# Hymba hybrid layer: the low parts of split weights from GpSimd to VectorE, SiLU as one ScalarE function, and the gate weights' split by ScalarE and VectorE

## The chip, the core and the metric

The kernel runs on one core of a Trainium2 chip. The core has a matrix engine (TensorE, PE in the profile, with its weight loads as PEld), three engines for elementwise work (VectorE, DVE; ScalarE, ACT; GpSimd, POOL), and SyncE (SP), whose queue issues nearly all DMA transfers here. Each engine works through its own queue in the order of the program and waits on semaphores for the others. The metric is the time of one execution on the device in microseconds (us), lower is better. The kernel before takes 1418.91 us, the median of three runs from 1418.45 to 1420.51.

## The reference

One decoder layer over 2048 positions of width 1024. The input `x` is RMS-normalised and multiplied by `w_in` (1024 x 6144). The six blocks of 1024 columns feed two mixers, a gated short convolution and a linear recurrence (RG-LRU); each output is normalised by heads, multiplied by the SiLU of its own gate block, and both together go through `w_out` (2048 x 1024), a residual addition and a last RMSNorm. All is float32.

```python
proj = jnp.einsum('bsd,de->bse', xn, w_in)
b_gate, c_gate, x_conv, g_conv, x_lru, g_lru = jnp.split(proj, splits, axis=-1)
y_conv = b_gate * causal_depthwise_conv(c_gate * x_conv, conv_w)
y_conv = headwise_rms_norm(y_conv, N_CONV_HEADS, conv_out_g) * jax.nn.silu(g_conv)
# rg_lru_mixer: u = conv(x_lru) + b
r = sigmoid(einsum('bshd,hde->bshe', uh, w_a) + b_a); i = sigmoid(einsum(..., w_i) + b_i)
log_a = 8.0 * r * log_sigmoid(lam); a = exp(log_a)
h_t = a_t * h_{t-1} + sqrt(-expm1(2 * log_a_t)) * (i_t * u_t)
y_lru = headwise_rms_norm(h, N_LRU_HEADS, lru_out_g) * jax.nn.silu(g_lru)
h = x + jnp.einsum('bse,ed->bsd', concat(y_conv, y_lru), w_out)
return rms_norm(h, final_g)
```

## The kernel before

**Products.** Each large product is done as a 2 x 2 block product with seven block products in place of eight (Winograd's form of Strassen's algorithm). So the weights of a step become seven combined blocks `S_0` to `S_6` (sums and differences of four loaded pieces `raw`), and the normalised activations, once per half of the sequence, seven combined blocks `T`. For precision each block is split in two: a high part, a cast to the matrix engine's fp32r format (`s` for weights, `th` for activations), and a low part, the float32 value less its high part (the second half of the `s` tile, and `tl`). A block product is then `sh*th + sh*tl + sl*th`, three matmuls for each of four pieces of depth: 12 matmuls of 128x512 (`mm`, L886), the **slot** in which the program is laid out.

**Steps.** The program goes through steps `n`, each of seven slots: for each block `k` of 128 columns an `l` step (`x_lru` and `g_lru`, consumer `lru`), an `a` step (`c_gate`, `x_conv`, `conv_a`) and a `b` step (`b_gate`, `g_conv`, `conv_b`); 24 steps for the first half of the sequence, 24 for the second, then 16 `o` steps for the output projection. Three steps `l`, `a`, `b` are called a period here. In steps 4 to 23 the split weights are also stored to DRAM (`sd`, L202), and the second half loads them again (`s_loads`, L218).

**The order.** The order on every engine is written by hand: instructions stand in the queues in the order in which the Python code makes them. `at(slots, f)` puts a function off by so many slots, `tick()`, called once a slot, runs those that are due. `s_plan` gives the eight pieces of work that make the next step's `S` blocks, one of which is done in each slot: `add` (a sum on VectorE), `hi` (ScalarE's cast, L197), `lo` (the low part, through `low` and `tt`, L160). In steps 4 to 23 (`PLAIN < n < 3 * KT`) the low parts 0, 4 and 6 are GpSimd's, the other four VectorE's. The store of a block follows its low part, by 3 slots where GpSimd made it and by 2 where VectorE did.

**Around the recurrence.** In `lru`, `sth` and `stl` split `u` into the tile `st`, `gates` lets TensorE multiply it by the split gate weights `bh` and `bl` into two small banks (`gate`, L666), `sigs` takes four sigmoids of them (L673) into `r` and `i`, for the first 512 columns and then for the second, which need the same two banks. Then come `tanh` (L682), `exp` (L685), a square root (L688), two products and the scan (L700). ScalarE holds one table set of functions at a time: sigmoid and tanh are in one, `exp` and the square root each need another, and the program has an ACT_TABLE_LOAD ahead of a function whose set isn't there.

**The SiLU.** `silu(g)` takes the sigmoid of a gate block into `sg` (ScalarE, L599) and two slots later multiplies it on GpSimd. `finish` later multiplies the normalisation gain, the mixer's output and this gate (L570). `load_gate_w` loads the gate weights and splits them with two GpSimd instructions (L615, L616).

**The banks.** The accumulated sums of a step lie in banks of PSUM, and ScalarE copies them out (`q`, `u`, `rr`, L1220 to L1226) or VectorE adds them to what was copied; the bank is free for TensorE after that. `u` (u2) is one tile, written again in each step, so its copy waits until VectorE has used the last one, which it does where it makes the last quarter of `gb` or `gl`.

Of the kernel before, what the change touches and what calls it, by code (L numbers as in the profile page):

```python
# [12 lines left out]
F32 = mybir.dt.float32  # L13
F32R = mybir.dt.float32r
AF = mybir.ActivationFunctionType
ALU = mybir.AluOpType
# [7 lines left out]
KT = D // P  # L24
# [14 lines left out]
def hymba_kernel(ctx: ExitStack, tc: tile.TileContext, x, xt, w_in, par, lamc, w_gate, w_out, final_g, out):  # L39
    nc = tc.nc  # L40
# [16 lines left out]
    sd = [dram.tile([7, P, 2, C], F32, name=f"sd{n}") for n in range(3 * KT)]  # L57
# [4 lines left out]
    def wt(tag, name, n=2 * C, dt=F32, bufs=1):  # L62
        return work.tile([P, n], dt, tag=tag, bufs=bufs, name=name)

    IG, O2, HL = 2, 2, 4
# [4 lines left out]
    def aux(name):  # L70
        return small.tile([P, C], F32, tag="aux", bufs=4, name=name)
# [69 lines left out]
    def at(slots, *fs):  # L141
        if slots == 0:
            for f in fs:
                f()
        else:
            due.append([slots, fs])
# [12 lines left out]
    def tt(out, a, b, op, eng=None):  # L159
        (eng or nc.vector).tensor_tensor(out=out, in0=a, in1=b, op=op)  # L160
# [6 lines left out]
    def low(v, hl, eng=None):  # L167
        tt(hl[1], v, hl[0].bitcast(F32), ALU.subtract, eng)
# [7 lines left out]
    def s_plan(n, r, dst):  # L176
        a11, a12, a21, a22 = r
        t, tiles = {}, {}

        def add(i):  # L180
            if i == 2:
                t[2] = aux("s1")
                tt(t[2], a21, a22, ALU.add)
            elif i == 1:
                t[1] = aux("s2")
                tt(t[1], t[2], a11, ALU.subtract)
            elif i == 3:
                tt(a21, a11, a21, ALU.subtract)
            else:
                tt(t[1], a12, t[1], ALU.subtract)  # L190

        def val(i):
            return {0: a11, 1: t.get(1), 2: t.get(2), 3: a21, 4: a12, 5: t.get(1), 6: a22}[i]

        def hi(i):
            tiles[i] = s_tile(dst, i)
            nc.scalar.copy(dst[i][0], val(i))  # L197

        def lo(i, eng=None):
            low(val(i), dst[i], eng)  # L200
            if PLAIN <= n < 3 * KT:
                at(3 if eng else 2, lambda: nc.sync.dma_start(sd[n][i], tiles[i].bitcast(F32)))  # L202

        g = nc.gpsimd if PLAIN < n < 3 * KT else None
        return [lambda: (add(2), add(1)),
                lambda: (hi(0), lo(0, g), add(3)),
                lambda: hi(1),
                lambda: (hi(3), lo(1)),
                lambda: (hi(2), lo(3), add(5)),
                lambda: (hi(4), lo(4, g), lo(2)),  # L210
                lambda: hi(5),
                lambda: (hi(6), lo(6, g), lo(5))]


    def s_loads(src, dst):
# [6 lines left out]
    PLAIN = 3  # L222
# [7 lines left out]
    class TPrep:  # L230
# [3 lines left out]
        def add(self, i):  # L234
            b11, b12, b21, b22 = (self.r.get(n) for n in range(4))
            t = self.t
            if i == 2:
                t[2] = aux("t1")
                tt(t[2], b12, b11, ALU.subtract)
            elif i == 1:  # L240
                t[1] = aux("t2")
                tt(t[1], b22, t[2], ALU.subtract)
            elif i == 3:
                tt(b12, b22, b12, ALU.subtract)
            else:
                tt(t[1], b21, t[1], ALU.subtract)
# [23 lines left out]
        def val(self, i):  # L270
            b11, b12, b21, b22 = (self.r.get(n) for n in range(4))
            return {0: b11, 1: self.t.get(1), 2: self.t.get(2), 3: b12, 4: b21, 5: b22,
                    6: self.t.get(1)}[i]

        def hi(self, i, v=None):
            self.dst[i, self.j] = hl = t_tile(self.dst, i, self.j)
            nc.scalar.copy(hl[0], self.val(i) if v is None else v)

        def lo(self, i, eng=None, v=None):
            low(self.val(i) if v is None else v, self.dst[i, self.j], eng)  # L280
# [311 lines left out]
        at(d0 + 7, lambda: hl_done(2))  # L592

    def silu(g, late=0):
        sg = [None]

        def f1():
            sg[0] = wt("ig", "sg", bufs=IG)
            nc.scalar.activation(out=sg[0], in_=g, func=AF.Sigmoid)  # L599

        at(2 + late, f1)
        at(4 + late, lambda: tt(g, g, sg[0], ALU.mult, nc.gpsimd))

# [2 lines left out]
    def load_gate_w(k):  # L608
        bd = aux("bd")[:, 0:2 * P].rearrange("p (h m) -> p h m", h=2)
        bh = small.tile([P, 2, P], F32R, tag="bh", name="bh")  # L610
        bl = small.tile([P, 2, P], F32R, tag="bl", name="bl")
        nc.sync.dma_start(bd, w_gate[k])

        def part():
            nc.gpsimd.tensor_scalar(out=bh, in0=bd, scalar1=1.0, scalar2=0.0, op0=ALU.mult, op1=ALU.add)  # L615
            nc.gpsimd.tensor_tensor(out=bl, in0=bd, in1=bh.bitcast(F32), op=ALU.subtract)  # L616

        at(3, part)
        return bh, bl
# [299 lines left out]
    g = nc.gpsimd  # L919
    with tc.manual_schedule(engines={ENG.PE, ENG.Activation, ENG.DVE, ENG.Pool, ENG.SP}):  # L920
# [176 lines left out]
        for n in range(PLAIN, N):  # L1097
# [53 lines left out]
            for s in range(8 if new or last else 7):  # L1151
                i = ((0, 6) + ORDER[1:])[s]
# [131 lines left out]
```

## Time and profile before

| | |
|---|---|
| median of three runs | 1418.91 us (1418.45 to 1420.51) |
| span of the profiled execution | 1418.1 us |
| TensorE, matmuls | 5732, mean 395 ns for 128x512 with `th` |
| VectorE busy | 1069.9 us |
| ScalarE busy | 782.6 us |
| GpSimd busy | 242.6 us, of it 118.9 in 62 low parts of weights (1931 ns each) and 87.6 in 32 products of the SiLU |
| ACT_TABLE_LOAD | 54 of 1283 ns |

The profile is of one execution; its span runs from the first to the last instruction, and nothing that is shown gives that execution's own time apart from it. The median of the runs lies 0.8 us above this span. A row of the time views has the start in us, the duration in us, engine, line, operation, output and inputs, shapes and count, and in brackets how long the engine had been idle and what ended that; a merged row (x2) has the time of all its instructions. A row of the waits view reads: who waited, for whom, us in total, times, longest. Matmuls overlap, and their listed durations are longer than the distance of their starts.

### The profile page before, as it was taken

To read this page: it belongs to the slowest core of one execution; us is meant where nothing else is said; L and a number is where in the kernel's file an instruction comes from. 1 tells how busy PE (TensorE), PEld (TensorE's weight loads), DVE (VectorE), ACT (ScalarE), POOL (GpSimd) and SP (SyncE) were. 2 spreads that over 40 slices of the span, in tenths; PEclk is the share of its full clock that TensorE was granted. 3 is DMA by queue.
4 is the path that set the end of the run, shared out by engine and by line. 5 is a ranking of instruction groups with operands and counts; after the bars stand their busy time and mean duration, and the time that the engine had idled before them with its cause. 6 is when DMAs were issued, how large, how long until landed. Compare 5 with 4: busy or idle time off the path is not lost.

```text
span 1418.1 us, 16977 instructions
## 1 busy us (share of the span) xinstructions
PE 1336.5 (94%) x5732; PEld 1072.3 (76%) x5732; DVE 1069.9 (75%) x1273; ACT 782.6 (55%) x1165; POOL 242.6 (17%) x159
## 2 busy tenths in 40 slices
PE   6989999999999997899998999998996999988997
PEld 5867777778777775677886878786874888867886
DVE  6778788898989989777767667665667647657885
ACT  7485757666566666375563645463656323343443
POOL 2104333433534430101000000101010000000000
PEclk9999999999999998999999999999997999999999
DMA  5147797898888865730899999998979998697643
GB/s 213 30 141 256 274 280 212 310 326 284 310 280 293 315 242 198 240 97 30 291 315 339 331 339 333 368 294 302 300 259 340 352 304 260 223 390 284 214 155 144
DMA packets 165191, 371.02 MB, mean 262 GB/s; under 512 B 17265, under 2 KB 52465, under 8 KB 165105
## 3 DMA queue, kind: packets, MB, share of 16 engines
q1 hardware_dynamic: 164816, 369.63, 76.3%
q8 instruction: 45, 0.74, 0.2%
q14 instruction: 42, 0.34, 0.1%
q10 hardware_dynamic: 288, 0.32, 0.1%
HBM read 224.45 MB, written 145.43 MB: 261 GB/s over the span
## 4 chain that ended last, share of the span: by engine, by line
PE 65%; DMA 13%; ACT 9%; DVE 8%; issue 3%; SPq 2%; POOL 0%; DVEq 0%; ACTq 0%; POOLq 0%
PE bank L886 60%; PE norm_ps L559 2%; DMA sd<-s 2%; ACT i L673 2%; ACT r L673 2%; PE gate L666 2%; DMA s<-so 2%; DVE s L160 2%; DVE tl L160 1%; DMA yd<-gl 1%; DMA zr<-rsd 1%; DVE traw L160 1%; DMA raw<-in_w_in_dram 1%; DMA traw<-in_w_out_dram 1%; DMA raw<-yd 1%
## 5 line engine op out<-in xcount | busy, mean ns | idle before, releaser
L886 PE MATMUL bank<-th,s 128*128 128x512 f32 x3608 | 1147.0, 395 | 41.5 <-DMA s<-so 9.8
L886 PEld LDWEIGHTS bank<-th,s 128*128 128x128 f32 x3608 | 685.3, 190 | 204.4 <-ACT u L1223 12.2
L886 PE MATMUL bank<-tl,s 128*128 128x512 f32 x1804 | 710.5, 394 | 6.3 <-DVE tl L160 6.0
L886 PEld LDWEIGHTS bank<-tl,s 128*128 128x128 f32 x1804 | 342.9, 190 | 81.4 <-DVE tl L160 10.4
L160 POOL TENSOR_TENSOR s<-raw,s 128x512 fp32r<-128x512 f32 x62 | 118.9, 1931 | 256.4 <-ACT s L197 180.2
L197 ACT CAST s<-raw 128x512 fp32r<-128x512 f32 x136 | 81.8, 616 | 59.6 <-PE bank L886 43.4
L1223 ACT COPY u<-bank 128x512 f32<-128x512 f32 x58 | 34.0, 587 | 141.3 <-PE bank L886 90.9
L160 DVE TENSOR_TENSOR s<-s,s 128x512 fp32r<-128x512 f32 x102 | 103.5, 1015 | 5.4 <-ACT s L197 5.4
L160 DVE TENSOR_TENSOR tl<-traw,th 128x512 fp32r<-128x512 f32 x102 | 70.0, 711 | 47.5 <-ACT th L454 29.1
L160 POOL TENSOR_TENSOR gb<-gb,sg 128x1024 f32<-128x1024 f32 x16 | 41.8, 2611 | 351.4 <-ACT sg L599 331.4
L160 DVE TENSOR_TENSOR s<-raw,s 128x512 fp32r<-128x512 f32 (+1 forms) x120 | 89.8, 771 | 9.9 <-ACT s L197 5.3
L1220 ACT COPY q<-bank 128x512 f32<-128x512 f32 x58 | 33.8, 583 | 79.2 <-PE bank L886 74.2
L160 DVE TENSOR_TENSOR raw<-raw,zr 128x512 f32<-128x512 f32 x64 | 49.6, 801 | 29.6 <-DMA zr<-rsd 29.6
L197 ACT CAST s<-s 128x512 fp32r<-128x512 f32 x102 | 62.8, 616 | 5.9 <-DVE s L160 5.9
L640 DVE SCALAR_TENSOR_TENSOR u<-xl,pt,u 128x1024 f32<-128x1024 f32 x48 | 64.5, 1344 | 0.8 <-ACT u L636 0.2
L1226 ACT COPY rr<-bank 128x512 f32<-128x512 f32 x58 | 33.9, 584 | 47.8 <-PE bank L886 47.7
L160 DVE TENSOR_TENSOR st<-u,st 64x1024 fp32r<-64x1024 f32 x32 | 52.0, 1626 | 1.0
L750 DVE SCALAR_TENSOR_TENSOR t<-p,pt,t 128x1024 f32<-128x1024 f32 x32 | 47.6, 1486 | 4.9 <-ACT t L747 4.1
L160 POOL TENSOR_TENSOR gl<-gl,sg 128x1024 f32<-128x1024 f32 x16 | 45.8, 2862 | 20.1 <-ACT sg L599 20.1
L160 DVE TENSOR_TENSOR ob<-bank,rr 128x512 f32<-128x512 f32 x18 | 12.2, 689 | 48.0 <-ACT rr L1226 48.0
L636 ACT ACTIVATE u<-xl,pt 128x1024 f32<-128x1024 f32 x16 | 19.9, 1245 | 46.8 <-DVE xl L160 46.8
L673 ACT ACTIVATE r<-gate,pt 64x512 f32<-64x512 f32 x64 | 43.8, 684 | 2.4 <-PE gate L666 1.8
(162 smaller groups left out, 1355.9 us busy)
## 6 DMA issues: line engine op xcount, KB each, us to landing
sd<-s SPq DMA_DIRECT2D x147, 512.0 KB, 4.8
s<-sd SPq DMA_DIRECT2D x147, 512.0 KB, 5.9
raw<-in_w_in_dram SPq DMA_DIRECT2D x108, 256.0 KB, 5.0
so<-so SPq DMA_DIRECT2D x42, 512.0 KB, 6.0
s<-so SPq DMA_DIRECT2D x42, 512.0 KB, 7.5
raw<-yd SPq DMA_DIRECT2D x64, 256.0 KB, 5.4
traw<-in_w_out_dram SPq DMA_DIRECT2D x56, 256.0 KB, 5.9
yd<-gl SPq DMA_DIRECT2D x32, 256.0 KB, 3.6
```

Source lines behind the costliest of these rows:

```text
L160: (eng or nc.vector).tensor_tensor(out=out, in0=a, in1=b, op=op)
L197: nc.scalar.copy(dst[i][0], val(i))
L559: nc.tensor.matmul(norm_ps[0], sel[:, s0:s0 + R], q[:, i * C:(i + 1) * C], start=norm_ps[1] == 0, stop=norm_ps[1] == 8 * KT - 1)
L636: nc.scalar.activation(out=v["u"], in_=o1[:, 1:1 + N2], func=AF.Identity, scale=lw[0], bias=pt[:, LB + k:LB + k + 1])
L640: nc.vector.scalar_tensor_tensor(out=v["u"], in0=o1[:, 1 + j:1 + j + N2], scalar=lw[j], in1=v["u"], op0=ALU.mult, op1=ALU.add)
L666: nc.tensor.matmul(ps[j], v["gw"][n][:, j, :], v["st"][j][:, sl], start=(n == 0), stop=(n == 1))
L673: nc.scalar.activation(out=g_[hi, sl], in_=v["ps"][j][src], func=AF.Sigmoid, bias=pt[src, bias + k:bias + k + 1])
L750: nc.vector.scalar_tensor_tensor(out=tcur["t"], in0=p[:, 2 + j:2 + j + N2], scalar=cw[j], in1=tcur["t"], op0=ALU.mult, op1=ALU.add)
L886: nc.tensor.matmul(bank, a[:, js], b, start=start and n == 0, stop=stop and n == 2, skip_group_check=more)
L1220: nc.scalar.copy(q1, bk["A"])
L1223: nc.scalar.copy(u2, bk["A"])
L1226: nc.scalar.copy(rr, bk["A"])
```

## The change

Three edits, all of which take work off GpSimd:

1. `lo` in `s_plan` is always VectorE's, so 60 low parts (0, 4 and 6 in steps 4 to 23) move from GpSimd to VectorE, and their stores to `sd` are issued 2 slots behind them and not 3.
2. `silu` is one ScalarE function in place, `Silu`; the tile `sg` and GpSimd's product go.
3. The gate weights' high part is a ScalarE cast and the low part a VectorE subtraction.

```diff
-        def lo(i, eng=None):
-            low(val(i), dst[i], eng)
+        def lo(i):
+            low(val(i), dst[i])
             if PLAIN <= n < 3 * KT:
-                at(3 if eng else 2, lambda: nc.sync.dma_start(sd[n][i], tiles[i].bitcast(F32)))
+                at(2, lambda: nc.sync.dma_start(sd[n][i], tiles[i].bitcast(F32)))
 
-        g = nc.gpsimd if PLAIN < n < 3 * KT else None
         return [lambda: (add(2), add(1)),
-                lambda: (hi(0), lo(0, g), add(3)),
+                lambda: (hi(0), lo(0), add(3)),
                 lambda: hi(1),
                 lambda: (hi(3), lo(1)),
                 lambda: (hi(2), lo(3), add(5)),
-                lambda: (hi(4), lo(4, g), lo(2)),
+                lambda: (hi(4), lo(4), lo(2)),
                 lambda: hi(5),
-                lambda: (hi(6), lo(6, g), lo(5))]
+                lambda: (hi(6), lo(6), lo(5))]
...
     def silu(g, late=0):
-        sg = [None]
-
-        def f1():
-            sg[0] = wt("ig", "sg", bufs=IG)
-            nc.scalar.activation(out=sg[0], in_=g, func=AF.Sigmoid)
-
-        at(2 + late, f1)
-        at(4 + late, lambda: tt(g, g, sg[0], ALU.mult, nc.gpsimd))
+        at(2 + late, lambda: nc.scalar.activation(out=g, in_=g, func=AF.Silu))
...
         def part():
-            nc.gpsimd.tensor_scalar(out=bh, in0=bd, scalar1=1.0, scalar2=0.0, op0=ALU.mult, op1=ALU.add)
-            nc.gpsimd.tensor_tensor(out=bl, in0=bd, in1=bh.bitcast(F32), op=ALU.subtract)
+            nc.scalar.copy(bh, bd)
+            tt(bl, bd, bh.bitcast(F32), ALU.subtract)
```

In the changed kernel the lines behind these edits have numbers that are 8 lower (the gate sigmoids are L665, the SiLU is L594).

TensorE's order is unchanged. ScalarE's queue around the gate sigmoids of an `l` step in the first half (`q` is the copy of a step's first bank, `p` a quarter of the next step's convolution input, `s` the high parts of weights), before:

```order
L729 COPY p<-bank 128x512
L197 CAST s<-s_2784 128x512
L1220 COPY q_2956<-bank 128x512
L673 ACTIVATE r<-gate,pt 64x512
L673 ACTIVATE i<-gate,pt 64x512
L673 ACTIVATE r<-gate,pt 64x512
L673 ACTIVATE i<-gate,pt 64x512
```

and after:

```order
L721 COPY p<-bank 128x512
L197 CAST s<-s_2769 128x512
L1212 COPY q_2938<-bank 128x512
L665 ACT_TABLE_LOAD
L665 ACTIVATE r<-gate,pt 64x512
L665 ACTIVATE i<-gate,pt 64x512
L665 ACTIVATE r<-gate,pt 64x512
L665 ACTIVATE i<-gate,pt 64x512
```

A table load stands between the copy of `q` and the first sigmoid. Such a load stands there in all 16 `l` steps, where before it stood in one, the first of the second half; the program has 69 loads in place of 54.

VectorE's queue around the scan of such a step (`s<-raw,s` and `s<-s_...,s` of 128x512 are low parts of weights, L691 and what follows belong to the recurrence, `xcol` is a normalised block of `x` for the second half), before:

```order
L691 SCALAR_TENSOR_TENSOR u<-r,u 128x1024
L160 TENSOR_TENSOR s<-s_2963,s 128x512
L160 TENSOR_TENSOR t<-bank,t 128x512
L160 TENSOR_TENSOR u<-T,u 128x1024
L700 SCALAR_TENSOR_TENSOR r<-r,u 128x1024
L703 COPY hl<-r 128x1
L520 SCALAR_TENSOR_TENSOR xcol<-xcol,pt 128x512
L160 TENSOR_TENSOR s_3146<-raw 128x512
L160 TENSOR_TENSOR s_3148<-s_3146,raw 128x512
L160 TENSOR_TENSOR gb<-bank,u_3014 128x512
L570 SCALAR_TENSOR_TENSOR gl<-r,pt,gl 128x1024
```

and after:

```order
L683 SCALAR_TENSOR_TENSOR u<-r,u 128x1024
L160 TENSOR_TENSOR s<-raw,s 128x512
L160 TENSOR_TENSOR s<-s_2946,s 128x512
L160 TENSOR_TENSOR t<-bank,t 128x512
L160 TENSOR_TENSOR u<-T,u 128x1024
L692 SCALAR_TENSOR_TENSOR r<-r,u 128x1024
L695 COPY hl<-r 128x1
L519 SCALAR_TENSOR_TENSOR xcol<-xcol,pt 128x512
L160 TENSOR_TENSOR s_3129<-raw 128x512
L160 TENSOR_TENSOR s_3131<-s_3129,raw 128x512
L160 TENSOR_TENSOR gb<-bank,u_2996 128x512
L569 SCALAR_TENSOR_TENSOR gl<-r,pt,gl 128x1024
```

One row is new within this stretch, the second, `lo(4)`; the others of a period's nine new low parts stand ahead of it and behind it.

## The prediction

> **What bounds the kernel now.** I read the page first, then who TensorE waits for, stage by stage, then the order of time around the gate sigmoids and around the scan, the two places that the diff touches.
>
> ```profile
> PE 1336.5 (94%) x5732; PEld 1072.3 (76%) x5732; DVE 1069.9 (75%) x1273; ACT 782.6 (55%) x1165; POOL 242.6 (17%) x159
> ```
>
> TensorE is busy 94% of the span, so another engine counts only where TensorE waits for it. The waits of TensorE from 104 to 530 us (steps 4 to 23, where GpSimd makes the low parts):
>
> ```profile
> PE bank L886 <- ACT u L1223: 4.6, 7, 1.0
> PE bank L886 <- ACT rr L1226: 1.7, 4, 1.2
> PE gate L666 <- ACT i L673: 1.2, 7, 0.2
> ```
>
> and from 700 to 990 us (second half of the sequence):
>
> ```profile
> PE norm_ps L559 <- DVE ql L160: 6.6, 4, 2.6
> PE bank L886 <- DMA s<-sd: 3.5, 4, 1.4
> PE bank L886 <- ACT q L1220: 2.8, 2, 1.4
> ```
>
> Two things are to be seen. In the first half TensorE waits 11 times for ScalarE's copies out of a bank, 6.3 us in all, and once in each period of three steps for the gate sigmoids. In the second half it loses twice as much, but for stores, loads and what hangs on them.
>
> **The new table load.** SiLU as one function isn't in the table set that holds the gate sigmoids: in the program order a load now stands in front of the first of them (none before, save once). The four sigmoids free the two small banks that the next gate matmuls need, and TensorE runs in order. A period without a load, ScalarE's copy first, then TensorE:
>
> ```profile
> 666.60 0.59 ACT L1220 COPY q<-bank 128x512 f32<-128x512 f32 x1 [2.58 <-PE bank L886]
> ...
> 668.90 0.39 PE L886 MATMUL bank<-th,s 128*128 128x512 f32 x1
> 669.94 0.50 PE L666 MATMUL gate<-st,bh 128*128 128x512 f32 x1 [0.18 <-ACT i L673]
> 670.51 0.39 PE L886 MATMUL bank<-th,s 128*128 128x512 f32 x1
> ```
>
> The copy waits for TensorE, the sigmoids follow it in ScalarE's queue, and the third row (0.18 us idle) shows that TensorE waits for the last of them already. So a load behind the copy has no cover: ScalarE's idle 2.58 us lie ahead of the copy, not behind it. And the trace holds the case with the load, once, because a square root has run in between:
>
> ```profile
> 603.79 0.59 ACT L1220 COPY q<-bank 128x512 f32<-128x512 f32 x1 [3.15 <-PE bank L886]
> 604.38 1.28 ACT L673 ACT_TABLE_LOAD   x1
> 605.68 0.68 ACT L673 ACTIVATE r<-gate,pt 64x512 f32<-64x512 f32 x1
> ...
> 606.04 0.39 PE L886 MATMUL bank<-th,s 128*128 128x512 f32 x1
> 607.12 0.50 PE L666 MATMUL gate<-st,bh 128*128 128x512 f32 x1 [0.69 <-ACT i L673]
> 608.52 0.50 PE L666 MATMUL gate<-st,bh 128*128 128x512 f32 x1 [0.67 <-ACT i L673]
> 609.09 0.39 PE L886 MATMUL bank<-th,s 128*128 128x512 f32 x1
> ```
>
> From the last matmul ahead of the gates to the first behind them TensorE needs 670.51 - 668.90 = 1.61 us without the load and 609.09 - 606.04 = 3.05 us with it: 1.44 us more. There are 16 `l` steps. One has the load already; in the very first,
>
> ```profile
> 79.58 0.68 ACT L673 ACTIVATE r<-gate,pt 64x512 f32<-64x512 f32 x1 [0.30 <-PE gate L666]
> ```
>
> ScalarE waits for TensorE just ahead of the sigmoids, and part of a load can run in that idle time; TensorE's wait list names none for `i` behind it. The other 14 pay: 14 x 1.44 = **+20.2 us**. The bounds of this term are 14 x 1.28 = 17.9 (the load alone) and 20.2.
>
> The Trainium skill ("ScalarE: Activation LUTs", What ACT_TABLE_LOAD costs) gives a switch of sets as 1283 ns and 1380 ns of drain, 2.66 us in all. By it the 14 loads would take 19 us more than I count and the forecast would be 1447; the trace has the 1.28 us, but no drain: the sigmoid starts 0.02 us behind the load at 605.66.
>
> **What GpSimd's work costs VectorE.** The scan stretch of a period in the first half, VectorE, then GpSimd and ScalarE, then two VectorE rows from moments without GpSimd:
>
> ```profile
> 351.24 0.68 DVE L160 TENSOR_TENSOR s<-s,s 128x512 fp32r<-128x512 f32 x1
> 352.44 2.15 DVE L160 TENSOR_TENSOR u<-T,u 128x1024 f32<-128x1024 f32 x1
> 354.62 2.29 DVE L700 TENSOR_TENSOR_SCAN r<-r,u 128x1024 f32<-128x1024 f32 x1
> 357.04 1.51 DVE L520 SCALAR_TENSOR_TENSOR xcol<-xcol,pt 128x512 f32<-128x512 f32 x1
> 358.47 1.77 DVE L160 TENSOR_TENSOR s<-raw 128x512 f32<-128x512 f32 x1
> 360.89 0.68 DVE L160 TENSOR_TENSOR gb<-bank,u 128x512 f32<-128x512 f32 x1
> ...
> 354.94 4.75 POOL L160 TENSOR_TENSOR s<-raw,s 128x512 fp32r<-128x512 f32 x2 [1.40 <-ACT s L197]
> ...
> 351.53 0.60 ACT L197 CAST s<-raw 128x512 fp32r<-128x512 f32 x1
> 361.66 0.59 ACT L1223 COPY u<-bank 128x512 f32<-128x512 f32 x1 [4.56 <-DVE gb L160]
> ...
> 361.49 1.28 DVE L570 SCALAR_TENSOR_TENSOR gl<-r,pt,gl 128x1024 f32<-128x1024 f32 x1
> 542.50 1.21 DVE L160 TENSOR_TENSOR u<-T,u 128x1024 f32<-128x1024 f32 x1
> ```
>
> Beside GpSimd, VectorE's 512-wide operations take 1.5 to 1.8 us in place of 0.68, the product 2.15 in place of 1.21 (the scan, which this GpSimd work should have met too, isn't longer than the 2.29 that I count on with): some 2.8 us in this stretch. They delay `gb`, the copy of `u` waits for `gb`, and TensorE for the bank. After the change one new low part, `lo(4)`, stands ahead of this stretch's `lo(2)` and `t`, and must wait for its cast (351.53 + 0.60). Counted on with clean durations (operations follow each other at 0.6 us): `lo(4)` ends at 352.8, `lo(2)` and `t` at 354.0, product 355.2, scan 357.5, `xcol` (taken at 0.7) 358.3, two sums 359.6, `gb` 360.2, where it was 361.57. The gain of 1.4 us is more than TensorE's wait in such a period. In the two periods with the longest waits the gain may be smaller, since VectorE waited for ScalarE there and `lo(4)` now stands behind that cast. The 11 waits are 6.3 us of idle time; as the gate rows show, a wait of 0.18 idle costs 0.35 from start to start, so they are worth some 6.3 + 11 x 0.17 = 8.2. I take three quarters, **-6.2 us**, and keep 0 and -8.2 as bounds. The 60 low parts that move to VectorE (20 steps of three, 0.68 us each at most, 41 us) lie where it is busy, but GpSimd's 2.4 us for each went largely into VectorE's own durations.
>
> Two collisions lie on the chain outside these steps, in the opening and at the change of halves:
>
> ```profile
> 64.09 2.62 DVE L160 TENSOR_TENSOR tl<-traw,th 128x512 fp32r<-128x512 f32 x1 [0.18 <-ACT th L1020]
> 63.63 2.54 POOL L160 TENSOR_TENSOR gl<-gl,sg 128x1024 f32<-128x1024 f32 x1 [5.38 <-ACT sg L599]
> 547.21 3.12 DVE L570 SCALAR_TENSOR_TENSOR gl<-r,pt,gl 128x1024 f32<-128x1024 f32 x1
> ```
>
> The first: 2.62 - 0.68 = 1.9 less, but the cast of `bh` now stands in ScalarE's queue ahead of the cast that feeds it (half the 512 columns that take 0.60, say 0.5): **-1.4 us**, bounds 0 and -1.9. The second: 3.12 - 1.28 = **-1.8 us**; TensorE waits for VectorE's and ScalarE's parts of the new activations there, bounds 0 and -1.8.
>
> **What I cost at nothing.** The SiLU takes the sigmoid's place at equal width, and GpSimd's product falls away; it is needed only many slots later. The gate weights:
>
> ```profile
> 783.56 0.41 POOL L615 TENSOR_SCALAR bh<-bd 128x256 fp32r<-128x256 f32 x1 [24.29 <-DMA bd<-in_w_gate_dram]
> 782.50 2.10 ACT L651 CAST st<-u 64x1024 fp32r<-64x1024 f32 x2
> ```
>
> GpSimd began when the weights landed, 783.56; ScalarE's new cast stands behind the two casts of `u`, which end at 784.60, so it waits for nothing. If the weights land over 1 us later, it holds ScalarE and the copy of `rr` behind it, 1 us or so a period, which TensorE feels only where that bank is needed at once. VectorE's subtraction waits for the cast, with `lo(1)`, `xx` and the low parts of `u` queued behind it, and the gate matmuls behind those; but these low parts shed their collisions with GpSimd too, which hides it. The stores of the 60 parts are issued a slot earlier, ahead of some loads in SP's queue; they wait there for VectorE in place of GpSimd, and TensorE doesn't wait for them in the first half.
>
> **In the second half** the transfers are near their limit:
>
> ```profile
> 104.00:530.00 426.00, 418.13 (x1813) 335.27 (x1812) 377.35 (x378) 279.63 (x409) 168.22 (x101) 1.00 0.83 281
> 700.00:990.00 290.00, 276.25 (x1190) 220.59 (x1189) 196.51 (x222) 143.66 (x189) 28.40 (x19) 0.99 0.96 331
> 605.05:608.47 3.42, 2.10 (x9) 1.09 (x7) 1.38 (x2) 3.34 (x5) 0.00 (x0) 1.00 0.94 329
> 1246.81:1250.22 3.41, 1.57 (x6) 0.67 (x4) 1.53 (x4) 1.86 (x3) 0.00 (x0) 1.00 1.04 397
> 1250.22:1253.64 3.42, 2.01 (x5) 1.67 (x6) 2.15 (x4) 1.85 (x3) 0.00 (x0) 0.50 1.04 408
> ```
>
> Each row has a stretch, its length, the busy time of TensorE, its weight loads, VectorE, ScalarE and GpSimd, the granted clock, the DMA share and GB/s. The DMA share is 0.96 from 700 to 990 us, where the first half (first row) has 0.83. A later TensorE lets queued transfers catch up, so part of four of the loads (4 x 1.44 = 5.8) comes back in shorter waits for them. But SP issues transfers in step with TensorE's slots, so most of it doesn't: **-1.5 us**, bounds 0 and -5.8.
>
> Sum: 20.2 - 6.2 - 1.4 - 1.8 - 1.5 = +9.3 us on a span of 1418.1. Nothing in the trace tells the profiled execution's own time; the median of the runs shown, 1418.9, lies 0.8 above this span, and I carry that over: 1428.
>
> **The rivals.**
> - *Not slower: everything that can come back does.* First half -8.2, opening -1.9, change of halves -1.8, transfers -5.8: 20.2 - 17.7 = +2.5, time 1421, which is the border of no change. The mechanism is the transfers: they decide if their queue is never empty between a gate and the stores behind it. For it: the share of 0.96. Against: SP's issue in step with TensorE. Chance 0.18.
> - *The load is not on the path* (it runs ahead of the copy, or isn't made): 9.3 - 20.2 = -10.9, 1408. Against: the rows at 604. 0.05.
> - *New waits for the old ones:* `lo(0)`, `lo(4)` and `lo(6)` follow their casts in the same slot, VectorE is held by ScalarE, and the first half gains nothing: 20.2 - 1.8 - 1.5 = +16.9, 1436. For it: 60 new waits in a queue that is 89% full (377.35 of 426 us); against: the count above. 0.13.
> - *The clock:* in the last two of these rows the granted clock falls to 0.50 behind a window in which TensorE was busy 1.57 of 3.41 us; with the load it was busy 2.10 (third row) and the clock stayed. If half of the 14 places fell below, each costs half of 3.41 us: 7 x 1.7 = +12, 1440. 0.05.
> - *The drain of the skill's page:* 1447, with 0.02, as the one measured load shows none.
>
> **How the numbers follow.** The forecast has 0.57. It and the rivals above it are slower by over 0.2% (2.8 us, about what a measurement of this kernel can tell): 0.57 + 0.13 + 0.05 + 0.02 = 0.77, less 0.02 for its own lower edge: 0.75. The first rival straddles the border and mostly counts as no change: 0.17. Faster: 0.08, the load off the path and a share of better recoveries than I see. The range runs from 1416 to 1438: below the full recovery, and over the case without gain in the first half; the clock, the drain and the load off the path, 0.12, are left out.
>
> **What would show it.** In the profile after: 16 loads at the line of the gate sigmoids in place of one, 15 more in all; TensorE's wait for `i` at the gates near 0.7 us twice per period in place of 0.18 once; VectorE's 512-wide low parts near 0.68 on the mean, its busy time lower though it has 76 instructions more; TensorE's waits for the copies of `u` and `rr` gone from the first half. Wrong would be: loads ahead of the copy, `lo` waits of VectorE on casts that reach TensorE, or a clock of 0.50 behind the gates.

## The result, and the profile after

| | before | after |
|---|---|---|
| median of four runs | 1418.68 us (1417.56 to 1420.51) | 1429.12 us (1428.02 to 1433.50) |
| span of the profiled execution | 1418.1 us | 1426.0 us |

The ratio is 1.0072, with a 95% interval from 1.0052 to 1.0091: slower, by some 10 us. The profiled execution of the changed kernel took 1428.28 us, 2.3 more than its span. In the runs of the kernel before that were timed beside the experiments, time and span lie 1.8 to 1.9 us apart. So the execution that was profiled before took some 1419.9 us, 1.2 above that kernel's median, and not the 1418.9 that the prediction carried over.

The low parts of weights that VectorE makes, in the page of the kernel before (groups of instructions: count, busy us, mean ns of one, idle us ahead of them and what ended it):

```profile
L160 DVE TENSOR_TENSOR s<-s,s 128x512 fp32r<-128x512 f32 x102 | 103.5, 1015 | 5.4 <-ACT s L197 5.4
L160 DVE TENSOR_TENSOR s<-raw,s 128x512 fp32r<-128x512 f32 (+1 forms) x120 | 89.8, 771 | 9.9 <-ACT s L197 5.3
```

In the page of the changed kernel, the busy time of each engine and the same two groups:

```profile
PE 1333.5 (94%) x5732; PEld 1068.3 (75%) x5732; DVE 1012.5 (71%) x1349; ACT 807.5 (57%) x1196; POOL 14.3 (1%) x35
...
L160 DVE TENSOR_TENSOR s<-raw,s 128x512 fp32r<-128x512 f32 (+1 forms) x180 | 123.6, 702 | 35.0 <-ACT s L197 29.4
L160 DVE TENSOR_TENSOR s<-s,s 128x512 fp32r<-128x512 f32 x102 | 69.8, 685 | 1.1 <-PE bank L878 0.6
```

VectorE has 76 instructions more and is busy 57.4 us less (1069.9 before). A low part takes 685 to 702 ns on the mean, where it took 771 to 1015: what VectorE took over costs less than the collisions with GpSimd did. It waits longer for the casts ahead of the low parts, 29.4 us where it was 10.7.

TensorE's longest sum of waits in the changed kernel, in the whole run:

```profile
PE gate L658 <- ACT i L665: 19.7, 30, 0.7
```

and from 104 to 530 us:

```profile
PE gate L658 <- ACT i L665: 9.2, 14, 0.7
PE bank L878 <- ACT u L1215: 1.4, 2, 0.8
PE bank L878 <- ACT rr L1218: 1.4, 2, 1.2
```

The waits for the copies of `u` and `rr` went from 4.6 and 1.7 us to 1.4 each; the wait at the gates went from 7 times 0.2 to 14 times 0.7. One such place in the order of time, ScalarE first, then TensorE:

```profile
332.42 0.59 ACT L1212 COPY q<-bank 128x512 f32<-128x512 f32 x1 [2.59 <-PE bank L878]
333.01 1.28 ACT L665 ACT_TABLE_LOAD   x1
334.31 0.68 ACT L665 ACTIVATE r<-gate,pt 64x512 f32<-64x512 f32 x1
...
334.71 0.39 PE L878 MATMUL bank<-th,s 128*128 128x512 f32 x1
335.74 0.50 PE L658 MATMUL gate<-st,bh 128*128 128x512 f32 x1 [0.64 <-ACT i L665]
337.14 0.50 PE L658 MATMUL gate<-st,bh 128*128 128x512 f32 x1 [0.67 <-ACT i L665]
337.71 0.39 PE L878 MATMUL bank<-th,s 128*128 128x512 f32 x1
```

Between the last matmul ahead and the first behind lie 337.71 - 334.71 = 3.00 us, where a period of before had 1.61. ScalarE's 2.59 us of idle time lie ahead of the copy, and the load behind it, with no cover.

**A ruler for the stages.** TensorE's order is the same in both kernels, so the start of the same matmul can be compared. I take the last `gate<-st,bl` of a group of gate matmuls, four times (of the first `l` step, of the last one of the first half, of the first group of the second half, and of the very last `l` step); in the order of time of the changed kernel

```profile
86.04 0.39 PE L658 MATMUL gate<-st,bl 128*128 128x512 f32 x1
525.87 0.40 PE L658 MATMUL gate<-st,bl 128*128 128x512 f32 x1
599.11 0.39 PE L658 MATMUL gate<-st,bl 128*128 128x512 f32 x1
1067.11 0.39 PE L658 MATMUL gate<-st,bl 128*128 128x512 f32 x1
```

(before: 87.84, 524.76, 600.56 and 1056.79). Their distances are the first half (seven `l` steps), the change of halves and the second half (eight `l` steps, the first of which had its load before). All kernels in us:

| kernel | opening, to the first mark | first half | change of halves | second half |
|---|---|---|---|---|
| before | 87.84 | 436.92 | 75.80 | 456.23 |
| after | 86.04 | 439.83 | 73.23 | 468.00 |
| load alone | 86.45 | 446.78 | 75.67 | 465.63 |
| load early | 85.94 | 429.78 | 73.29 | 456.56 |
| load early, again | 87.30 | 429.75 | 73.82 | 456.80 |
| low parts alone | 87.82 | 432.39 | 74.96 | 462.17 |
| SiLU alone | 85.16 | 445.60 | 73.88 | 469.41 |
| gate weights alone | 88.17 | 437.16 | 75.47 | 458.28 |
| product on VectorE | 87.83 | 429.88 | 73.46 | 464.83 |
| product behind `ql` | 87.36 | 429.81 | 75.61 | 459.74 |
| product on GpSimd | 87.64 | 431.73 | 74.44 | 456.42 |
| GpSimd, full dose | 87.08 | 445.83 | 74.42 | 455.65 |
| GpSimd, half dose | 87.52 | 436.71 | 74.04 | 455.05 |

The first half is a fine measure: the three kernels in which GpSimd has next to no work and no load is added on the path (one of them profiled twice) agree within 0.13 us. The opening is not (the same kernel gives 85.94 and 87.30). For the second half it isn't known: the one kernel that was profiled twice repeats it within 0.24 us, but single executions of one kernel differ by 3 to 13 us, and if the first half always repeats so well, that lies in the other stages. A profile is one execution, too: that of the low parts alone is the slowest of ten and that of the product on GpSimd the fastest of ten, each some 4 us from its median. From before to after the four columns change by -1.8, +2.9, -2.6 and +11.8, and what follows the last mark (the last `a` and `b` steps and the `o` steps) by -2.4: together +7.9, the difference of the spans.

The same can be done for every single matmul: the distance of its start from the start of the one ahead of it, in one kernel less in the other. These differences add up to a column's and tell where it arose. Below, "from start to start" means this count.

### The profile page after: what moved, and what is told of

It reads as the page before. It is cut to its first block, busy times and chain, and to the rows that moved or that the text cites. A ratio compares the mean times of both kernels' runs of the same rounds, so it can differ in the third digit from the quotient of the medians.

```text
span 1426.0 us, 16810 instructions
## 1 busy us (share of the span) xinstructions
PE 1333.5 (94%) x5732; PEld 1068.3 (75%) x5732; DVE 1012.5 (71%) x1349; ACT 807.5 (57%) x1196; POOL 14.3 (1%) x35
## 4 chain that ended last, share of the span: by engine, by line
PE 68%; DMA 11%; ACT 10%; DVE 7%; issue 2%; SPq 1%; POOL 0%; DVEq 0%; ACTq 0%
PE bank L878 64%; DMA traw<-in_w_out_dram 2%; DMA yd<-gl 2%; PE gate L658 2%; ACT i L665 2%; ACT r L665 2%; PE norm_ps L558 2%; DMA s<-sd 1%; DVE tl L160 1%; ACT L665 1%; DMA raw<-yd 1%; DVE traw L160 1%; DVE s L160 1%; DMA sd<-s 1%; DMA so<-so 1%
## 5 line engine op out<-in xcount | busy, mean ns | idle before, releaser
L160 DVE TENSOR_TENSOR s<-raw,s 128x512 fp32r<-128x512 f32 (+1 forms) x180 | 123.6, 702 | 35.0 <-ACT s L197 29.4
L160 DVE TENSOR_TENSOR s<-s,s 128x512 fp32r<-128x512 f32 x102 | 69.8, 685 | 1.1 <-PE bank L878 0.6
L160 DVE TENSOR_TENSOR raw<-raw,zr 128x512 f32<-128x512 f32 x64 | 43.0, 688 | 37.7 <-DMA zr<-rsd 37.6
L658 PE MATMUL gate<-st,bh 128*128 128x512 f32 x64 | 28.9, 452 | 24.5 <-ACT i L665 19.7
L160 DVE TENSOR_TENSOR gl<-bank,rr 128x512 f32<-128x512 f32 x15 | 10.4, 691 | 56.4 <-DMA yd<-gl 44.7
L453 ACT CAST th<-traw 128x512 fp32r<-128x512 f32 x56 | 33.1, 619 | 22.6 <-DMA traw<-in_w_out_dram 9.7
L160 DVE TENSOR_TENSOR xx<-bank,u 128x512 f32<-128x512 f32 x15 | 10.4, 691 | 49.1 <-PE bank L878 49.1
L665 ACT ACTIVATE r<-gate,pt 64x512 f32<-64x512 f32 x64 | 43.8, 684 | 1.9 <-PE gate L658 1.1
L721 ACT COPY p<-bank 128x512 f32<-128x512 f32 x17 | 10.0, 588 | 61.3 <-PE bank L878 58.6
L665 ACT ACTIVATE i<-gate,pt 64x512 f32<-64x512 f32 x64 | 43.8, 684 | 1.0
```

The costliest lines, as they stand in the source:

```text
L453: nc.scalar.copy(self.dst[i, j][0], self.r[i, j])
L658: nc.tensor.matmul(ps[j], v["gw"][n][:, j, :], v["st"][j][:, sl], start=(n == 0), stop=(n == 1))
L665: nc.scalar.activation(out=g_[hi, sl], in_=v["ps"][j][src], func=AF.Sigmoid, bias=pt[src, bias + k:bias + k + 1])
L721: nc.scalar.copy(dst, bank)
```

## The experiments

**The load alone.** The kernel before, with a `Silu` of one column in each `l` step, a slot ahead of the gate sigmoids, so that the sigmoids' set must be loaded again:

```diff
-                for slots, *fs in ((5, sth), (6, stl), (8, lambda: gates(0)), (9, lambda: sigs(0)),
+                for slots, *fs in ((5, sth), (6, stl), (8, lambda: gates(0), lambda: nc.scalar.activation(out=warm, in_=eps, func=AF.Silu)), (9, lambda: sigs(0)),
```

> The kernel before, in which nothing leaves GpSimd, with one thing added: a tiny SiLU of 128x1 in the slot ahead of the gate sigmoids, so that its table load falls into ScalarE's idle time there and 15 of the 16 sigmoid groups have a load of their own set ahead of them. Theory (the load between the copy of q and the sigmoids is what costs): 14 places x 1.44 us = +20 us, so 1418.7 + 20 = 1439 us, and TensorE waits for i twice a period for 0.7 us. Rival (the change is slower through new work and waits on VectorE, and the load is mostly covered): within 3 us of 1418.7.

Measured: 1438.30 us, ratio 1.0141 [1.0120, 1.0161], 19.4 us above before. TensorE's waits in this kernel's whole run:

```profile
PE gate L666 <- ACT i L673: 19.8, 30, 0.7
```

The same 30 waits as in the changed kernel. The first half is 9.86 us longer, 1.41 for each of seven loads, the second 9.40 for another seven. From start to start the gate matmuls themselves account for 9.8 us in each half, 1.40 for each load; the remaining -0.4 of the second half isn't clear of what one profile can tell.

**The load early.** The changed kernel, with a `Sigmoid` of one column a slot ahead of the gate sigmoids. The number of loads stays, they move up in ScalarE's queue:

```diff
-                for slots, *fs in ((5, sth), (6, stl), (8, lambda: gates(0)), (9, lambda: sigs(0)),
+                for slots, *fs in ((5, sth), (6, stl), (8, lambda: gates(0), lambda: nc.scalar.activation(out=warm, in_=eps, func=AF.Sigmoid)), (9, lambda: sigs(0)),
```

> The changed kernel with a tiny sigmoid of 128x1 in the slot ahead of the gate sigmoids: the same 69 loads, but the 16 of the sigmoid's set one slot earlier, where ScalarE waits for TensorE. Theory: the 20 us of the loads on the path go and what was gained from GpSimd's collisions stays, 1429.1 - 20.2 = 1409 us, about 10 us below the kernel before. Rival (the moves to VectorE cost as much as they free): 1419 us, as before; rival (the load's time matters wherever it stands, as ScalarE's total): 1429 us, no change.

Measured: 1407.93 us, ratio 0.9924 [0.9906, 0.9941]; run once more beside other kernels:

> The variant with the early load once more, on the same chip as the two above, for comparison with them: 1406 to 1410 us, as before.

Measured: 1409.92 us, ratio 0.9937 [0.9917, 0.9957]. It is faster than both kernels. The same period as above in the order of time, ScalarE, then TensorE, of the first of these two runs:

```profile
324.75 1.28 ACT L710 ACT_TABLE_LOAD   x1
326.05 0.20 ACT L710 ACTIVATE warm<-eps 128x1 f32<-128x1 f32 x1
326.16 0.60 ACT L197 CAST s<-s 128x512 fp32r<-128x512 f32 x1
327.84 0.59 ACT L1212 COPY q<-bank 128x512 f32<-128x512 f32 x1 [1.08 <-PE bank L878]
328.32 0.69 ACT L665 ACTIVATE r<-gate,pt 64x512 f32<-64x512 f32 x1
...
330.13 0.39 PE L878 MATMUL bank<-th,s 128*128 128x512 f32 x1
331.16 0.50 PE L658 MATMUL gate<-st,bh 128*128 128x512 f32 x1 [0.17 <-ACT i L665]
331.73 0.40 PE L878 MATMUL bank<-th,s 128*128 128x512 f32 x1
```

The load runs in the idle time ahead of the copy, of which 1.08 us are still left. TensorE needs 331.73 - 330.13 = 1.60 us, as in the kernel before. Against the changed kernel the first half is 439.83 - 429.78 = 10.05 us shorter, 1.44 for each of seven loads. The load that before had in the second half went off the path too.

**The low parts alone** (the first edit on the kernel before, whose diff stands above).

> The kernel before with the 60 low parts alone moved to VectorE; SiLU and gate weights stay as they were, so no load is added. Theory (each collision cost VectorE about as much as the part itself, and the waits behind gb go): the 7 us that came back between the gates of the first half, 1418.7 - 7 = 1412 us, TensorE's waits for u and rr from 104 to 530 us down from 6.3 to about 3 us. Rival (new waits of VectorE on casts eat it): 1417 to 1420 us.

Measured: 1414.38 us, ratio 0.9972 [0.9957, 0.9987], a little less gain than expected. TensorE's waits from 104 to 530 us:

```profile
PE bank L885 <- ACT rr L1225: 2.4, 3, 1.2
PE gate L665 <- ACT i L672: 1.3, 7, 0.2
PE bank L885 <- ACT u L1222: 1.1, 2, 0.6
```

The waits for `u` mostly go (4.6 before), those for `rr` don't. The first half is 4.5 us shorter. `gl` at the change of halves is as slow as before:

```profile
L569 DVE SCALAR_TENSOR_TENSOR gl<-r,pt,gl x1: 3120/3120/3120, 542.7 to 542.7; 128x1024 f32<-128x1024 f32 x1
```

**The SiLU alone** (the second edit on the kernel before).

> The kernel before with SiLU alone as one ScalarE function; low parts and gate weights stay on GpSimd. Theory: the loads, +20.2 us, less the two collisions with GpSimd's products on the chain (-1.9 in the opening, -1.8 to -2.6 at the change of halves), 1418.7 + 16 = 1435 us. Rival (what was gained back in the changed kernel came from the products that left, not from the low parts): 1428 to 1430 us, as the whole change.

Measured: 1432.17 us, ratio 1.0092 [1.0070, 1.0115], 3 us below the expectation and 2 above the rival's. The same `gl` (a row gives shortest, median and longest of one instruction in ns, here one):

```profile
L570 DVE SCALAR_TENSOR_TENSOR gl<-r,pt,gl x1: 1276/1276/1276, 553.2 to 553.2; 128x1024 f32<-128x1024 f32 x1
```

So it was GpSimd's product of the SiLU that slowed `gl`; the change of halves is 1.9 us shorter. The first half is 8.7 longer: from start to start 9.8 at the gates, for seven loads, less 1.1 elsewhere, 1.0 of it at the copies of `u`, where products no longer collide.

**The gate weights alone** (the third edit on the kernel before).

> The kernel before with the third edit alone (the gate weights' split by ScalarE and VectorE). Theory of the prediction, that it costs nothing: 1418 to 1419 us, the same as before, and TensorE's waits for the copies of rr from 104 to 530 us within 1 us of those before (1.7). Rival, from the sum of the parts (the whole change is 10.4 us slower, the first edit alone was 4.5 faster and the second 13.3 slower, so 1.6 are left): 1420 to 1421 us, with the waits for rr up by 1 to 2 us because the cast of bh or its wait for the weights stands ahead of that copy.

Measured: 1420.75 us, ratio 1.0017 [1.0005, 1.0028], 2.4 us slower. But the waits for `rr` are those of before:

```profile
PE bank L886 <- ACT rr L1226: 1.8, 4, 1.2
```

The rival had the time right and its reason wrong. In this profile the first half is 0.24 us longer and the second 2.1, but its span is that of before (1418.0), so it doesn't show the loss; where the 2.4 us come from stays open. The three parts give -4.0, +13.1 and +2.4 (ratio less one, times 1418.7), together +11.5, the whole +10.2 with an interval from 7.4 to 12.9: they add up within what is known of them.

**The SiLU as a sigmoid, with the product on VectorE.** The changed kernel, without any added load and without work on GpSimd:

```diff
-        at(2 + late, lambda: nc.scalar.activation(out=g, in_=g, func=AF.Silu))
+        at(2 + late, f1)
+        at(4 + late, lambda: tt(g, g, sg[0], ALU.mult))
```

(`f1` takes the sigmoid into `sg`, as before.)

> The changed kernel, but with the SiLU as a sigmoid on ScalarE and a product on VectorE; so no work is left on GpSimd and no table load is added. Theory (the loads are the whole cost, VectorE has room for 32 products of 1.2 us, 39 us): 1429.1 - 14 x 1.40 = 1409.5 us, waits at the gates near 0.2 us once per period. Rival (VectorE's added 39 us stand ahead of the parts that TensorE waits for): 1413 to 1418, with the waits for the copies of u and rr back to 3 us or more from 104 to 530 us.

Measured: 1416.69 us, ratio 0.9995 [0.9977, 1.0013]. A miss: 7 us over the expectation, and not by the rival's reason, since the waits for `u` and `rr` stay low and the first half is as short as with the early load. The loss is in the second half. TensorE's longest sum of waits there, from 700 to 990 us:

```profile
PE norm_ps L558 <- DVE ql L160: 10.6, 4, 3.8
```

and the longest of the four, TensorE's row first, then VectorE's in the order of time:

```profile
830.41 0.46 PE L558 MATMUL norm_ps<-ql,sel 128*64 128x512 f32 x1 [3.80 <-DVE ql L160]
827.40 0.69 DVE L160 TENSOR_TENSOR gl<-bank,rr 128x512 f32<-128x512 f32 x1 [7.09 <-DMA yd<-gl]
828.01 1.21 DVE L160 TENSOR_TENSOR gb<-gb,sg 128x1024 f32<-128x1024 f32 x1
829.14 1.22 DVE L160 TENSOR_TENSOR ql<-r,qh 128x1024 fp32r<-128x1024 f32 x1
```

VectorE's first row waits for a store, `gl` to DRAM; the product stands behind it in the queue and ahead of `ql`, for which TensorE waits. VectorE had been idle for 7 us. A product that costs 1.2 us in a queue with room is on the path because of its place.

These waits are only a part of the loss. Just behind this one (stretch, length, busy times of TensorE, its weight loads, VectorE, ScalarE and GpSimd, then the granted clock, DMA share and GB/s):

```profile
830.80:834.00 3.20, 3.20 (x9) 2.42 (x8) 3.13 (x6) 0.29 (x1) 0.00 (x0) 0.50 0.50 202
```

The granted clock is 0.50, and matmuls start 0.43 us apart there where they otherwise start 0.23 apart. This trace has four such stretches of 3.4 us in its second half, behind waits of 1.9 to 3.8 us; the early load has none there. From start to start, the second half is 8.3 us longer than with the early load: 5.0 for longer waits for `ql`, 5.8 for matmuls at the lower clock, 1.4 for the one load that the early load had taken off the path and this kernel keeps, less 3.4 for waits for copies of `q` that fall away and 0.5 for shorter waits of other kinds.

**The same product one slot later**, behind `ql`: `at(5 + late, ...)` in place of `at(4 + late, ...)`.

> The SiLU as sigmoid on ScalarE and product on VectorE again, with the product one slot later, so that it stands behind ql and the two low parts in VectorE's queue. Theory (in the second half the product stood between the add that waits for the store of gl and ql, for which TensorE waits: 1.14 us in each of five or so periods, and more where the transfers fall in behind it): 1409 to 1412 us, TensorE's waits for ql from 700 to 990 us back from 10.6 to 5 or 6 us. Rival (VectorE has no room for the products at any place): 1415 to 1418 as before the move.

Measured: 1415.06 us, ratio 0.9975 [0.9959, 0.9990]: 3 us above the expectation, in the rival's range, and not clear of the earlier place, whose interval overlaps this one. TensorE's waits for `ql` from 700 to 990 us:

```profile
PE norm_ps L558 <- DVE ql L160: 5.3, 4, 1.3
```

The wait for `ql` is back to that of the early load (5.8 in its second run), and the second half 5.1 us shorter; so VectorE has room for the products there. But the change of halves is 2.2 us longer than with the earlier place, and the time is only 1.6 lower. The place again: at the change of halves the earlier product had run at 548.99 us, where VectorE would have waited for ScalarE; the later one starts at 557.10, ahead of the low part `tl` of the new activations for which TensorE waits. That wait goes from 1.07 to 2.27 us, and the clock behind it is 0.50 for 6.8 us in place of 3.4.

**The same product on GpSimd**, the first and third edit without the second:

```diff
-        at(2 + late, lambda: nc.scalar.activation(out=g, in_=g, func=AF.Silu))
+        at(2 + late, f1)
+        at(4 + late, lambda: tt(g, g, sg[0], ALU.mult, nc.gpsimd))
```

> The changed kernel with the old SiLU (sigmoid on ScalarE, product on GpSimd), that is edits one and three without the second. Theory (the parts add up; the 32 products still collide with VectorE in the opening and at the change of halves, and now and then in the periods): 1429.1 - 13.3 = 1416 us, at most 1418, so 4 to 7 us above the version with the product on VectorE. Rival (GpSimd's products cost VectorE nothing that TensorE feels): the same time as with the product on VectorE, within 2 us.

Measured: 1414.79 us, ratio 0.9974 [0.9962, 0.9986]. GpSimd's product costs 1.9 us in the first half against VectorE's (431.73 to 429.88), and 1.0 at the change of halves. The expectation had the time (1416), but not the 4 to 7 us above the product on VectorE: it is 1.9 lower, as the rival had it within 2 us. The rival's reason is wrong, since GpSimd's product does cost the first half; it is no slower in total, because it doesn't stand in front of `ql`: TensorE's waits for `ql` from 700 to 990 us are 5.5 us, where VectorE's product has 10.6.

**GpSimd work that nobody waits for.** The early-load variant, with GpSimd subtracting from a dead tile wherever it made a low part before: the full dose with four 128x128 operations, the half dose with two.

```diff
             low(val(i), dst[i])
+            if PLAIN < n < 3 * KT and i in (0, 4, 6):
+                for c in range(0, C, P):
+                    tt(ident, ident, dst[i][0].bitcast(F32)[:, c:c + P], ALU.subtract, nc.gpsimd)
```

(in the half dose `for c in (0, P):`)

> The variant with the early load (1407.9 us), with GpSimd work added beside VectorE that nothing waits for: in steps 4 to 23, where GpSimd once made the low parts 0, 4 and 6, it subtracts the block's high part from a dead tile, as four 128x128 operations. Theory (the relief of the first half came from GpSimd's work stretching VectorE's operations): VectorE's low parts of 128x512 grow from 0.69 us to near 1.0 on the mean again, the waits for the copies of u and rr from 104 to 530 us return to 4 us or more, and the time goes up by 4 to 7 us, to 1412 to 1415. Rival (the relief came from what waited for GpSimd's own late results): VectorE's durations and TensorE's waits stay, 1408 us.

> The variant with the early load and GpSimd work that nothing waits for, but two 128x128 operations per place in place of four, some 1.8 us each time, which is about what one low part took on GpSimd (1.93). Theory (GpSimd's work stretches VectorE's operations, in proportion to its time): between the early load alone (1407.9) and the full dose (1426.0), 1413 to 1418 us, with the waits for the copies of u from 104 to 530 us at 3 to 6 us, as in the kernel before. Rival (the full dose did harm only because GpSimd fell behind and held blocks of weights): 1408 to 1410, waits for u near 1 us.

Measured: 1426.01 us, ratio 1.0050 [1.0033, 1.0066], with the full dose (11 us more than I expected at most) and 1414.08, ratio 0.9971 [0.9959, 0.9983], with half of it (inside what I expected). From 104 to 530 us, full dose, the groups of GpSimd's work and of VectorE's low parts:

```profile
L160 POOL TENSOR_TENSOR ident<-ident,s 128x128 f32<-128x128 f32 x236 | 210.0, 890 | 234.1 <-ACT s L197 212.2 <-issue 6.3
L160 DVE TENSOR_TENSOR s<-raw,s 128x512 fp32r<-128x512 f32 x80 | 67.5, 844 | 15.9 <-ACT s L197 13.9 <-DMA raw<-in_w_in_dram 1.8
```

and TensorE's wait for `u`:

```profile
PE bank L881 <- ACT u L1218: 10.7, 6, 2.0
```

The same groups and the same wait with the half dose:

```profile
L160 POOL TENSOR_TENSOR ident<-ident,s 128x128 f32<-128x128 f32 x120 | 108.8, 907 | 337.4 <-ACT s L197 331.2
L160 DVE TENSOR_TENSOR s<-raw,s 128x512 fp32r<-128x512 f32 x81 | 62.4, 770 | 18.3 <-ACT s L197 16.2 <-DMA raw<-in_w_in_dram 1.8
```

```profile
PE bank L881 <- ACT u L1218: 5.0, 6, 1.1
```

and with none (the early load, first run):

```profile
L160 DVE TENSOR_TENSOR s<-raw,s 128x512 fp32r<-128x512 f32 x81 | 55.6, 687 | 20.1 <-ACT s L197 19.9
```

```profile
PE bank L878 <- ACT u L1215: 1.1, 2, 0.6
```

No result of GpSimd is used, and yet the low parts grow from 687 to 770 to 844 ns and the waits for `u` from 1.1 to 5.0 to 10.7 us. The first half goes from 429.78 to 436.71 to 445.83. With the half dose, from start to start, 6.8 of the 6.9 us arise where TensorE waits for the copies of `u` (4.9) and `rr` (1.8). That its first half lies within 0.3 us of the 436.92 of the kernel before is in part luck: GpSimd was busy for 168 us there from 104 to 530 us, products included, and for 109 here. The Trainium skill ("SBUF — State Buffer", Who interferes with whom) says that VectorE shares one pair of its ports with GpSimd, and that whoever holds it locks the other out; these rows agree, in that work whose results nobody uses slows VectorE.

GpSimd reads a block's high part, so it might hold the block and keep ScalarE from the next cast. ScalarE's idle time ahead of these casts, half dose:

```profile
ACT s L197 <- issue: 11.2, 7, 1.9
ACT s L197 <- PE bank L881: 8.8, 10, 1.6
```

and none:

```profile
ACT s L197 <- PE bank L878: 20.7, 17, 1.6
```

It is 20.0 and 20.7 us in 17 waits each (for seven of the half dose the profile names nothing that ended them), so at this dose blocks held by GpSimd cost ScalarE nothing that shows, and the rival falls. At the full dose it is 23.1 us; there a part of the loss may be of this kind.

## Why the prediction was right, step by step

- **The load on the path, +20.2** (14 times 1.44): shown. The load alone gives +19.4 for the kernel; from start to start the gates account for 19.6 us in it and for 19.2 in the changed kernel. Taken off the path a load gives back 1.44. The first of all, in the opening, costs TensorE nothing: there are 16 loads and 30 waits, two for each of the other 15. The rival that the load isn't on the path needs a load ahead of the copy, which the early load had to be given by hand.
- **The first half, -6.2** (bounds 0 and -8.2): the mechanism is shown, the size was a little short. Without the loads the first half is 436.92 - 429.78 = 7.1 us shorter. From start to start 4.8 of it lie at the copies of `u` and 1.8 at those of `rr`, where the prediction had put it. It counted a wait at its idle time and 0.17 us and took three quarters of that; but a wait here also costs 0.11 us at the next matmul (one of 0.41 us idle costs 0.57 and 0.11). By edits, the low parts alone bring 4.5; the third edit on top of them 0.7 (432.39 to 431.73); and the products the remaining 1.9. That collisions alone suffice for this, without a wait for GpSimd's results, is what the GpSimd work that nobody waits for shows. The stretch around the scan that the prediction counted through reads in the changed kernel:

```profile
352.62 0.69 DVE L160 TENSOR_TENSOR s<-raw,s 128x512 fp32r<-128x512 f32 x1 [0.83 <-ACT s L197]
...
354.44 1.22 DVE L160 TENSOR_TENSOR u<-T,u 128x1024 f32<-128x1024 f32 x1
355.69 2.29 DVE L692 TENSOR_TENSOR_SCAN r<-r,u 128x1024 f32<-128x1024 f32 x1
...
360.11 0.68 DVE L160 TENSOR_TENSOR gb<-bank,u 128x512 f32<-128x512 f32 x1
```

  `lo(4)` waits 0.83 us for its cast, the product takes 1.22 again, and `gb` ends at 360.79. TensorE stands 0.51 us later here than before (the last gate matmul ahead of the stretch, 337.48 against 336.97), so that is 360.3 by the old clock; the count gave 360.2.
- **New waits for the old ones** (rival, 1436): VectorE's waits for the casts did grow, from 10.7 to 29.4 us in all, but not on TensorE's path, as the first half shows. The sign that the prediction gave, that TensorE's waits for the copies of `u` and `rr` would be gone from the first half, came only in part: 2.8 of 6.3 us are left.
- **The opening, -1.4:** not to be settled. The first mark lies 1.8 us earlier, but that of the load alone, which has no relief in it, 1.4, and two runs of one kernel differ by as much.
- **The change of halves, -1.8:** measured -2.6. The SiLU alone gives 1.9, so the term itself was right; the low parts alone give another 0.8 there, which I hadn't counted (one kernel profiled twice differs by 0.5 in this stage).
- **The second half, -1.5, the wrong step.** "A later TensorE lets queued transfers catch up" has no support. The second half is longer by 9.4 us with the load alone, by 11.8 in the changed kernel and by 13.2 with the SiLU alone, and from start to start 9.8, 9.7 and 9.7 of that are the gates. So the loads cost their full price, and the rest of the stage gives back 0.4 at most and otherwise adds to it. TensorE's waits for `s<-sd` from 700 to 990 us, which were to shrink, went from 3.5 to 4.6 us in the changed kernel. With this step falls the first rival, whose price rested on 5.8 us from it. The DMA share of 0.96 was no sign that time lost elsewhere returns.
- **Where the sum comes out:** it was +9.3 on the span, and the spans differ by 7.9; the medians by 10.4. The 2.5 us between are known: the execution profiled before was 1.2 us above its median, the one after 0.8 below, and time and span lie 0.5 further apart in the changed kernel. The 0.8 us that the prediction put between span and time was mis-sized. That the total came so near is in part luck. By stages the prediction had -1.4, +3.9, -1.8, +8.6 and nothing behind the last mark, and these profiles have -1.8, +2.9, -2.6, +11.8 and -2.4: its second half is 3 us too short, and a last stage for which it had no term makes up most of that.
- **The clock** (rival, 1440): not seen at the gates, where TensorE waits no longer than 0.7 us at a time. At the gates of the changed kernel and just behind them (columns as above):

```profile
334.30:337.70 3.40, 2.09 (x8) 1.12 (x7) 1.38 (x2) 3.32 (x5) 0.00 (x0) 1.00 0.91 274
337.70:341.10 3.40, 3.40 (x16) 2.82 (x15) 2.29 (x4) 2.00 (x4) 0.00 (x0) 1.00 0.39 73
```

  Its trace has no stretch at 0.50 from 81 to 551 us nor from 576 to 1091, so at none of the other gates either, save those of the opening. What the rival feared is real elsewhere: behind longer waits it cost the product on VectorE 5.8 us.

- **The drain** that the Trainium skill ("ScalarE: Activation LUTs", What ACT_TABLE_LOAD costs) adds to a load isn't in this trace: the sigmoid begins 0.02 us after the load's end (334.31 against 333.01 + 1.28), and a whole load costs TensorE 1.40 to 1.44 us. Nor is it at 67 of the 69 loads of the changed kernel, behind which the next instruction begins within 0.02 us.
- **The gate weights, nothing:** alone they cost 2.4 us (0.7 to 4.0), by a route that no run here shows.

## What to carry to other kernels

When a function moves to another table set, look at what stands ahead of the next use of the old set: where the engine's idle time came behind the load, the load cost nothing here, where it lay ahead, the load cost its full time, and an instruction of one column, placed ahead of the idle time, moved the load there (a change of +10 us became one of -9 to -11). Work on GpSimd isn't free just because nobody waits for it: price it by what VectorE's durations beside it become. An instruction is cheap or dear by its place in the queue, not by how busy its engine is. And look at the granted clock behind long waits of TensorE: in one variant here, behind waits of 1.9 to 3.8 us, the slower matmuls cost as much as the longer waits.

## What I hadn't expected

- A table load waits for nothing but its turn: the one for the one-column sigmoid ran as soon as ScalarE had come to it, and the sigmoids a few instructions later, in the same set, needed none.
- GpSimd's cost to the kernel grows faster than its time: 109 us of it cost the first half 6.9 us, 210 us cost 16.1. VectorE's low parts don't show this (83 ns longer on the mean, then 157); why the path feels more of it wasn't traced.
- GpSimd took 907 ns for 128x128 (half dose) and 1931 for 128x512 (the low parts before): four times the data for 2.1 times the time.
- The stages repeat very differently: the first half within 0.13 us over four profiles of three kernels, the opening only within 1.4 over two profiles of one.
